# Turning the gated activations of a feed-forward: TensorE transposes replaced by VectorE blocks and two DMA transfers

## The chip, the cores and the metric

The kernel runs on one core of a Trainium2 chip. The metric is the device time of one execution in microseconds. Three runs of the kernel before took 1472.68, 1473.67 and 1474.22 us; their median, 1473.67 us, is the time before. One further execution was taken with the hardware profiler; every row of a profile below is from that one.

## The reference, cut to what matters

Two layers of an encoder, each of four blocks in a row: a feed-forward, a mixer of three attention-like branches, a cross-attention, and a second feed-forward. There are 256 tokens of width 1024; all data is fp32. The change touches the feed-forward alone, which is run four times:

```
def swiglu(h, w13, w2):
    gate, up = jnp.split(h @ w13, 2, axis=-1)
    return (jax.nn.silu(gate) * up) @ w2

h = rms_norm(x, ffn1_norms[l, 0])
x = x + 0.5 * rms_norm(swiglu(h, ffn1_w13[l], ffn1_w2[l]), ffn1_norms[l, 1])
```

with w13 of shape (1024, 5632) and w2 of shape (2816, 1024). The product silu(gate) * up, a matrix of 256 tokens by 2816, has its tokens on the partitions when it is computed; the product with w2 sums over the 2816 and so needs them on the partitions.

## The kernel before, in words

The 256 tokens are two tiles of 128 (i = 0, 1). Every fp32 product is made of three matmuls: each operand is split into a high part h and a low part l (`split`: ScalarE writes h as a rounded copy, VectorE writes l = value - h), and `mm3` adds h·h, h·l and l·h in PSUM. These are lines 210, 211 and 215, and nearly all of TensorE's work; one such matmul has 128 rows of weights and 512 columns.

The weights come from one stream in DRAM, in blocks of 128 x 1024. `load` takes a block: the SP queue brings it into `raw` (4 buffers), ScalarE makes `wh` (line 156) and VectorE `wl` (line 157), 8 buffers each. A block is used by 12 matmuls, then its buffers come free for the block eight further on.

A feed-forward (`ffn`) goes over the 2816 in six chunks: chunk 0 of 256 columns, chunks 1 to 5 of 512. In a chunk, `gemm_chunk` makes gate (4 blocks, 24 matmuls for each i) and up (the same). Then `gated` computes `s` = silu(gate) on ScalarE (line 363) and `g` = up * s on VectorE (line 365), and defers to the next `tick` the call `into_T`: TensorE transposes `g` in pieces of 128 x 128 (line 262; four for a chunk of 512, two for one of 256) into PSUM, from which `split` makes `gTh` and `gTl`. After up of chunk c come the rows of w2 of chunk c - 1, which use `gT` of chunk c - 1: four blocks of 12 matmuls. Behind chunk 5 stands `finish`: eight rows of w2 are left, of chunks 4 and 5. Two are done for both i (24 matmuls), and then the last six together for i = 0 and then for i = 1, for each half n of the output; the rows of chunk 4 come first in each. `boundary` then makes the norm and the new x.

A scheduler orders the instructions of each engine by dependence and priority when the kernel is built, and sets the waits. Each engine runs its own instructions strictly in that order, a DMA that it issues included.

Of the kernel before, what the change touches and what calls it, by code (L numbers as in the profile page):

```python
# [11 lines left out]
F32 = mybir.dt.float32  # L12
# [8 lines left out]
P = 128  # L21
# [33 lines left out]
def _ffn_blocks(f, l):  # L55
    w13, w2 = f"{f}_w13", f"{f}_w2"
    out = {("w13", 0): _chunk(w13, (l,), [(2560, 2816), (D_FF + 2560, D_FF + 2816)]), ("w2", 0): [_kn(w2, (l,), k, 1, [(0, D)]) for k in (20, 21)]}
    for c in range(1, 6):
        o = (c - 1) * 512
        out["g", c] = _chunk(w13, (l,), [(o, o + 512)])  # L60
        out["u", c] = _chunk(w13, (l,), [(D_FF + o, D_FF + o + 512)])
        out["w2", c] = [_kn(w2, (l,), 4 * (c - 1) + k, 1, [(0, D)]) for k in range(4)]
    return out
# [3 lines left out]
    return [_kn(name, idx, k, 1, [(0, D)]) for k in range(nk)]  # L67


def _lay(inputs, blk):  # L70
    name, idx, k0, nk, cols = blk
    w = inputs[name][idx]
    parts = [w[k0 * P:(k0 + nk) * P, a:b].reshape(nk, P, b - a) for a, b in cols]
    a = np.concatenate(parts, axis=2) if len(parts) > 1 else parts[0]
    return np.ascontiguousarray(a.transpose(1, 0, 2)).reshape(-1)
# [28 lines left out]
def hybrid_encoder(ctx: ExitStack, tc: tile.TileContext, stream: Stream, t: dict, out: bass.AP):  # L104
    nc = tc.nc
# [6 lines left out]
    wk = ctx.enter_context(tc.tile_pool(name="wk", bufs=2))  # L112
    st = ctx.enter_context(tc.tile_pool(name="st", bufs=48))
    xp = ctx.enter_context(tc.tile_pool(name="xp", bufs=1))
    pps = ctx.enter_context(tc.tile_pool(name="pps", bufs=8, space=PSUM))

    def ps_tile():
        return pps.tile([P, 512], F32, tag="ps", name="ps")
# [34 lines left out]
    def split(h, l, src, scale=None):  # L153

        if scale is None:
            nc.scalar.activation(h, src, AF.Copy)  # L156
            nc.vector.tensor_tensor(out=l, in0=src, in1=h.bitcast(F32), op=ALU.subtract)  # L157
        else:
            nc.scalar.activation(h, src, AF.Copy, scale=scale)
            nc.vector.scalar_tensor_tensor(out=l, in0=src, scalar=scale, in1=h.bitcast(F32), op0=ALU.mult, op1=ALU.subtract)  # L160

    def load(blk):

        blk = _freeze(blk)
        w = _blk_width(blk)
        off = stream.place(blk)
        raw = wp.tile([P, w], F32, tag="raw", name="raw", padded_shape=[P, BLK])
        nc.sync.dma_start(out=raw, in_=ws[off:off + P * w].rearrange("(p e) -> p e", p=P))
        h = hp.tile([P, w], F32R, tag="wh", name="wh", padded_shape=[P, BLK])
        l = hp.tile([P, w], F32R, tag="wl", name="wl", padded_shape=[P, BLK])  # L170
        split(h, l, raw)
        nk = blk[3]
        return (h.rearrange("p (k n) -> p k n", k=nk), l.rearrange("p (k n) -> p k n", k=nk))
# [3 lines left out]
    def defer(fn, pieces=1):  # L177

        queue.append(fn if pieces == 1 else lambda: defer(fn, pieces - 1))

    def tick():
        due = queue[:]
        queue.clear()
        for fn in due:
            fn()
# [31 lines left out]
    def gemm_chunk(o, aT, blocks, j0=0, total=None, low_last=False):  # L217

        tiles = [(bh[:, k, :], bl[:, k, :]) for bh, bl in blocks for k in range(bh.shape[1])]
        total = total or len(tiles)  # L220
        for k, (bh, bl) in enumerate(tiles):
            j = j0 + k
            if low_last:
                mm2(o, aT[0][:, j, :], bh, bl, j == 0)
            else:
                mm3(o, aT[0][:, j, :], aT[1][:, j, :], bh, bl, j == 0, j == total - 1)
        for k, (bh, bl) in enumerate(tiles if low_last else []):
            nc.tensor.matmul(o, lhsT=aT[1][:, j0 + k, :], rhs=bh, start=False, stop=j0 + k == total - 1)  # L228
        tick()

    def lead(blks_a, use_a, blks_b, use_b, beside=lambda n: None):

        a = []
        for n, k in enumerate(blks_a):
            a.append(load(k))
            beside(n)
        o0, p0 = ps_tile(), ps_tile()
        gemm_chunk(o0, xT[0], a, low_last=True)
        use_a(0, o0)
        b = [load(k) for k in blks_b[:2]]  # L240
        gemm_chunk(p0, xT[0], b, 0, KD)
        o1 = ps_tile()
        gemm_chunk(o1, xT[1], a)
        use_a(1, o1)
        b += [load(k) for k in blks_b[2:]]
        gemm_chunk(p0, xT[0], b[2:], 4, KD)
        use_b(0, p0)
        p1 = ps_tile()
        gemm_chunk(p1, xT[1], b)
        use_b(1, p1)  # L250

    def gemm_rows(o, n, aT, j, blk, first, last):

        bh, bl = blk
        c = slice(n * 512, n * 512 + 512)
        mm3(o, aT[0][:, j, :], aT[1][:, j, :], bh[:, 0, c], bl[:, 0, c], first, last)

    def transposes(src, n, rows=P):

        p = ps_tile()  # L260
        for i in range(n):
            nc.tensor.transpose(p[:rows, i * P:(i + 1) * P], src[:, i * rows:(i + 1) * rows], ident)  # L262
        return p
# [6 lines left out]
    def into_T(dst, j0, src, nblk, scale=None):  # L270

        p = transposes(src, nblk)
        pv = p[:, :nblk * P].rearrange("p (k t) -> p k t", k=nblk)
        split(dst[0][:, j0:j0 + nblk, :], dst[1][:, j0:j0 + nblk, :], pv, scale)
# [46 lines left out]
    def new_accs():  # L321
        return [[ps_tile() for _ in range(2)] for _ in range(NT)]
# [32 lines left out]
    def ffn(f, l, r, pg, ng, early=lambda n: None, beside=lambda: None):  # L355
        b = _ffn_blocks(f, l)
        with tc.tile_pool(name="ff", bufs=2) as ff:
            gT = {}

            def gated(i, c, gate, up):  # L360
                w = gate.shape[1]
                s = ff.tile([P, 512], F32, tag="s", name="s")
                nc.scalar.activation(s[:, :w], gate, AF.Silu, scale=r[i])  # L363
                g = ff.tile([P, 512], F32, tag="g", name="g")
                nc.vector.scalar_tensor_tensor(out=g[:, :w], in0=up, scalar=r[i], in1=s[:, :w], op0=ALU.mult, op1=ALU.mult)  # L365
                nk = w // P
                gT[c, i] = d = tuple(ff.tile([P, 4, P], F32R, tag=f"gT{p}", name=f"gT{p}", bufs=5) for p in "hl")
                defer(lambda: into_T(d, 0, g, nk))

            gate = {}  # L370

            def use_gate(c):
                def use(i, o):
                    gate[c, i] = o
                return use

            lead(b["w13", 0], lambda i, o: gated(i, 0, o[:, :256], o[:, 256:]), b["g", 1], use_gate(1), early)
            accs = new_accs()
            for c in range(1, 6):
                if c > 1:  # L380
                    blocks = [load(k) for k in b["g", c]]
                    for i in range(NT):
                        gate[c, i] = ps_tile()
                        gemm_chunk(gate[c, i], xT[i], blocks)
                blocks = [load(k) for k in b["u", c]]
                for i in range(NT):
                    o = ps_tile()
                    gemm_chunk(o, xT[i], blocks)
                    gated(i, c, gate[c, i], o)
                if c < 5:  # L390
                    for n, k in enumerate(b["w2", c - 1]):
                        blk = load(k)
                        for i in range(NT):
                            for h in range(2):
                                gemm_rows(accs[i][h], h, gT[c - 1, i], n, blk, c == 1 and n == 0, False)
                        tick()
                if c == 2:
                    beside()
            work = []
            for c in (4, 5):  # L400
                aT = [gT[c, i] for i in range(NT)]
                work += [(aT, n, k) for n, k in enumerate(b["w2", c])]
            return finish(accs, work, pg, ng, 4.0)
# [579 lines left out]
    for l in range(DEPTH):  # L983
        g = {k: t[f"{k}_norms"][l] for k in ("ffn1", "mix", "cross", "ffn2")}
        r = ffn("ffn1", l, r, g["ffn1"][1], g["mix"][0], *((early, rope_tables) if l == 0 else ()))
        r, mem = mixer(l, r, g["mix"][1], g["cross"][0])
        r = cross(l, r, mem, g["cross"][1], g["ffn2"][0])
        r = ffn("ffn2", l, r, g["ffn2"][1], t["ffn1_norms"][l + 1, 0] if l + 1 < DEPTH else None)
# [61 lines left out]
```

## Time and profile before

| | before |
|---|---|
| median of three runs | 1473.67 us |
| the profiled execution | 1472.88 us |
| its span in the profile | 1471.1 us |
| TensorE busy | 1452.0 us, 99% |
| VectorE busy | 895.7 us, 61% |
| ScalarE busy | 755.9 us, 51% |
| DMA of the main queue, share of 16 engines | 54.9% |
| transposes of g (line 262) | 176 |

A row of the profile names a line, an engine, an operation and its tiles as out<-in with their shapes. PE is TensorE's matmul, PEld its weight load, which runs beside the matmul before; DVE is VectorE, ACT ScalarE, POOL GpSimd, SPq the queue of SyncE. Matmuls overlap in the profile: each is shown 0.39 us long, and the next one starts 0.23 us after it, so the distance of two starts is what one costs, not its length.

### The profile page before, as it was taken

The page shows a single profiled execution, that of the slowest core. Times are in us where ns is not written, and L with a number is a line of the kernel's source. Part 1 is how long each engine was busy: PE and PEld are TensorE (multiplying, and loading weights), DVE is VectorE, ACT ScalarE, POOL GpSimd, SP SyncE. Part 2 cuts the span into 40 slices and gives each one's busy share as a digit, 9 for nine tenths or more (in the row PEclk, how much of TensorE's full clock was granted, in tenths as well). Part 3 has the DMA queues.
Part 4 walks back from the last instruction along what each step waited for, and adds up shares of the span by engine and source line. Part 5 has one row for each costly group of instructions (what it writes and reads, how often), then busy time and mean ns, then how long its engine had stood idle before and what let it go on. Part 6 is the DMA issues. An engine that isn't in the chain of part 4 may idle for free.

```text
span 1471.1 us, 18753 instructions
## 1 busy us (share of the span) xinstructions
PE 1452.0 (99%) x6988; PEld 1209.8 (82%) x6988; DVE 895.7 (61%) x1154; ACT 755.9 (51%) x1096; POOL 91.6 (6%) x192
## 2 busy tenths in 40 slices
PE   7999999999999999999999999999999999999998
PEld 6888888888788888888888888888887888888886
DVE  6655567465776657554575554765666866664553
ACT  6444455664546546444464443666554656554442
POOL 0000022100201001000000000221002010100000
PEclk9999999999999999999999999999999999999999
DMA  8656656444456527555466554655444664465561
GB/s 287 208 182 199 194 183 199 159 160 137 141 200 229 171 96 246 203 191 186 145 231 209 189 187 157 211 181 170 144 161 131 205 234 131 146 217 182 175 198 56
DMA packets 75756, 266.03 MB, mean 181 GB/s; under 512 B 8909, under 2 KB 10893, under 8 KB 75661
## 3 DMA queue, kind: packets, MB, share of 16 engines
q1 hardware_dynamic: 75664, 264.83, 54.9%
q8 instruction: 55, 0.90, 0.3%
q14 instruction: 37, 0.30, 0.1%
HBM read 263.75 MB, written 1.05 MB: 180 GB/s over the span
## 4 chain that ended last, share of the span: by engine, by line
PE 91%; DVE 3%; DMA 1%; ACT 1%; POOL 1%; issue 1%; SPq 0%; POOLq 0%; DVEq 0%; ACTq 0%
PE ps L210 28%; PE ps L211 28%; PE ps L215 28%; PE ps L262 4%; DMA raw<-in_ws 1%; DVE wl L157 1%; PE ps L761 1%; PE ps L781 1%; PE ps L228 1%; POOL st L143 0%; ACT wh L156 0%; PE ps L773 0%; ACT e L487 0%; DVE tg L583 0%; PE ps L934 0%
## 5 line engine op out<-in xcount | busy, mean ns | idle before, releaser
L157 DVE TENSOR_TENSOR wl<-raw,wh 128x1024 fp32r<-128x1024 f32 x478 | 577.2, 1217 | 310.7 <-ACT wh L156 296.7
L156 ACT ACTIVATE wh<-raw 128x1024 fp32r<-128x1024 f32 x478 | 502.0, 1056 | 372.7 <-PE ps L215 323.0
L210 PE MATMUL ps<-wh,xTh 128*128 128x512 f32 (+1 forms) x1312 | 519.0, 396 | 0.5 <-ACT mem L156 0.5
L211 PE MATMUL ps<-wl,xTh 128*128 128x512 f32 (+1 forms) x1312 | 511.4, 390 | 1.9 <-DVE wl L157 1.9
L215 PE MATMUL ps<-wh,xTl 128*128 128x512 f32 (+1 forms) x1264 | 491.7, 389 | 0.0
L211 PEld LDWEIGHTS ps<-wl,xTh 128*128 128x128 f32 x1312 | 247.4, 189 | 51.3 <-DVE wl L157 3.6
L210 PEld LDWEIGHTS ps<-wh,xTh 128*128 128x128 f32 x1312 | 247.3, 189 | 50.2 <-ACT mem L156 0.9
L215 PEld LDWEIGHTS ps<-wh,xTl 128*128 128x128 f32 x1264 | 237.2, 188 | 49.3 <-DVE xTl L160 0.2
L210 PE MATMUL ps<-wh,gTh 128*128 128x512 f32 x352 | 141.3, 401 | 0.0
L215 PE MATMUL ps<-wh,gTl 128*128 128x512 f32 x352 | 137.5, 391 | 0.0
L211 PE MATMUL ps<-wl,gTh 128*128 128x512 f32 x352 | 137.0, 389 | 0.0
L215 PEld LDWEIGHTS ps<-wh,gTl 128*128 128x128 f32 x352 | 66.0, 188 | 14.5
L211 PEld LDWEIGHTS ps<-wl,gTh 128*128 128x128 f32 x352 | 66.3, 188 | 12.5
L210 PEld LDWEIGHTS ps<-wh,gTh 128*128 128x128 f32 x352 | 66.2, 188 | 12.2
L363 ACT ACTIVATE s<-ps,st 128x512 f32<-128x512 f32 (+1 forms) x48 | 31.4, 654 | 82.1 <-PE ps L215 78.7
L300 POOL TENSOR_SCALAR st<-st 128x1 f32<-128x1 f32 x16 | 4.8, 302 | 969.3 <-ACT junk L294 969.3
L365 DVE SCALAR_TENSOR_TENSOR g<-ps,st,s 128x512 f32<-128x512 f32 (+1 forms) x48 | 33.7, 703 | 49.1 <-PE ps L215 48.4
L296 DVE TENSOR_TENSOR t<-ps,gain 128x512 f32<-128x512 f32 x32 | 22.0, 689 | 56.4 <-ACT junk L294 56.4
L487 ACT ACTIVATE e<-ps,st 128x256 f32<-128x256 f32 (+1 forms) x80 | 33.5, 430 | 34.6 <-DVE st L485 34.6
L210 PE MATMUL ps<-wh,mem 128*128 128x512 f32 x128 | 51.0, 398 | 0.0
L215 PE MATMUL ps<-wh,mem 128*128 128x512 f32 x128 | 50.0, 390 | 0.0
L211 PE MATMUL ps<-wl,mem 128*128 128x512 f32 x128 | 49.9, 390 | 0.0
(202 smaller groups left out, 1302.4 us busy)
## 6 DMA issues: line engine op xcount, KB each, us to landing
raw<-in_ws SPq DMA_DIRECT2D x466, 512.0 KB, 4.3
gain<-in_ffn_norms SPq DMA_DIRECT2D x7, 512.0 KB, 5.4
raw<-in_ws SPq DMA_DIRECT2D x8, 416.0 KB, 5.2
gain<-in_mix_norms SPq DMA_DIRECT2D x4, 512.0 KB, 4.9
gain<-in_cross_norms SPq DMA_DIRECT2D x4, 512.0 KB, 5.1
m<-in_mem SPq DMA_DIRECT2D x4, 512.0 KB, 3.6
raw<-in_ws SPq DMA_DIRECT2D x4, 384.0 KB, 3.0
tmpb<-in_c_decay SPq DMA_DIRECT2D x8, 192.0 KB, 3.4
```

Source lines behind the costliest of these rows:

```text
L156: nc.scalar.activation(h, src, AF.Copy)
L157: nc.vector.tensor_tensor(out=l, in0=src, in1=h.bitcast(F32), op=ALU.subtract)
L210: nc.tensor.matmul(o, lhsT=ah, rhs=bh, start=first, stop=False)
L211: nc.tensor.matmul(o, lhsT=ah, rhs=bl, start=False, stop=False)
L215: nc.tensor.matmul(o, lhsT=al, rhs=bh, start=False, stop=last)
L228: nc.tensor.matmul(o, lhsT=aT[1][:, j0 + k, :], rhs=bh, start=False, stop=j0 + k == total - 1)
L262: nc.tensor.transpose(p[:rows, i * P:(i + 1) * P], src[:, i * rows:(i + 1) * rows], ident)
L296: nc.vector.tensor_tensor(out=tt[h], in0=y[h], in1=pg[:, cc], op=ALU.mult)
L363: nc.scalar.activation(s[:, :w], gate, AF.Silu, scale=r[i])
L365: nc.vector.scalar_tensor_tensor(out=g[:, :w], in0=up, scalar=r[i], in1=s[:, :w], op0=ALU.mult, op1=ALU.mult)
L487: nc.scalar.activation(e[:, h, :w], s[:, j, :], AF.Exp, bias=nm[:, h:h + 1], accum_out=sums[:, h:h + 1])
L761: nc.tensor.matmul(s[h], lhsT=qT[i][:, 4 * g + h, :], rhs=kT[:, 4 * g + h, :w], start=True, stop=True)
```

## The change

`gated` no longer defers `into_T`; it calls `turn`. VectorE transposes `g` in blocks of 32 x 32 into `gB`. ScalarE's queue writes `gB` to a tile `far` in DRAM (128 rows of 2 KB for a chunk of 512). At the next tick the same queue reads `far` back into `gM` with rows and pieces exchanged (for each partition four pieces of 512 bytes), and at the tick after that `split` makes `gTh` and `gTl` from `gM`, in SBUF. In `gT` the 128 features of a block stand in another order than before; on the host, the rows of w2 are put in the same order (`_turned`). TensorE's transposes in other parts of the kernel stay.

```
+def _turned(w):
+    n = w.shape[-1]
+    return w.reshape(-1, 4, 32, n).transpose(0, 2, 1, 3).reshape(-1, n)
...
+    if name in ("ffn1_w2", "ffn2_w2"):
+        w = _turned(w)
...
+    dram = ctx.enter_context(tc.tile_pool(name="dram", bufs=4, space=bass.MemoryType.DRAM))
...
+            def turn(dst, src, nk):
+                b = ff.tile([P, 512], F32, tag="gB", name="gB")[:, :nk * P]
+                nc.vector.transpose(b.rearrange("p (c k t) -> p k c t", c=4, t=32), src.rearrange("p (k c j) -> p k c j", k=nk, c=4))
+                far = dram.tile([4, P, nk, 32], F32, tag=f"far{nk}", name="far")
+                nc.scalar.dma_start(out=far.rearrange("a (j c) k t -> (a j) (c k t)", c=4), in_=b)
+
+                def back():
+                    m = ff.tile([P, 512], F32, tag="gM", name="gM")[:, :nk * P].rearrange("p (a e) -> p a e", a=4)
+                    nc.scalar.dma_start(out=m, in_=far.rearrange("a q k t -> q a (k t)"))
+                    h, l = (d[:, :nk, :].rearrange("p k (a t) -> p a k t", a=4) for d in dst)
+                    defer(lambda: split(h, l, m.rearrange("p a (k t) -> p a k t", t=32)))
+                defer(back)
...
-                defer(lambda: into_T(d, 0, g, nk))
+                turn(d, g[:, :w], nk)
```

The scheduler's order on TensorE at the end of the first feed-forward, before: the four transposes of `g` of chunk 5, i = 0, stand between the last matmul of up (on xT) and the first of w2's row (on gT); line 262 is the transpose.

```order
L211 MATMUL ps<-wl,xTh_90 128x512
L215 MATMUL ps<-wh,xTl_91 128x512
L262 MATMUL ps<-ident,g 128x128 [waits DVE_49,Activation_49]
L262 MATMUL ps<-ident,g 128x128 x3
L210 MATMUL ps<-wh,gTh 128x512 [waits Activation_49]
```

The same place on TensorE after (the lines are 9 further down in the file):

```order
L220 MATMUL ps<-wl,xTh_92 128x512
L224 MATMUL ps<-wh,xTl_93 128x512
L219 MATMUL ps<-wh,gTh 128x512 [waits Activation_49]
L220 MATMUL ps<-wl,gTh 128x512 [waits DVE_49]
L224 MATMUL ps<-wh,gTl 128x512
```

The transposes are gone; the matmuls around them keep their order, here and (but for two single matmuls that change places with a neighbour) in the whole program.

ScalarE's order at the same place, from the silu of chunk 5, i = 1, to the first square of `boundary` (line 294 before, 303 after), before:

```order
L363 ACTIVATE s_1426<-ps_1314,st_227 128x512
L156 ACTIVATE wh_1487<-raw_1485 128x1024
L156 ACTIVATE wh_1493<-raw_1491 128x1024
L156 ACTIVATE wh_1499<-raw_1497 128x1024
L156 ACTIVATE wh_1505<-raw_1503 128x1024
L156 ACTIVATE wh_1511<-raw_1509 128x1024
L156 ACTIVATE gTh_1392<-ps_1419 128x512
L156 ACTIVATE wh_1698<-raw_1696 128x1024
L156 ACTIVATE gTh_1430<-ps_1454 128x512
L156 ACTIVATE wh_1704<-raw_1702 128x1024
L294 ACTIVATE junk_1534,st_1533<-ps_320 128x512
```

After, at the same place:

```order
L165 ACTIVATE wh_1511<-raw_1509 128x1024
L377 DMA far_1412<-gB_1410 128x512
L165 ACTIVATE wh_1517<-raw_1515 128x1024
L165 ACTIVATE wh_1523<-raw_1521 128x1024
L381 DMA gM_1439<-far_1412 128x4x128
L165 ACTIVATE wh_1529<-raw_1527 128x1024
L165 ACTIVATE gTh_1408<-gM_1439 128x4x4x32
L165 ACTIVATE wh_1716<-raw_1714 128x1024
L377 DMA far_1449<-gB_1447 128x512
L165 ACTIVATE wh_1722<-raw_1720 128x1024
L381 DMA gM_1475<-far_1449 128x4x128
L165 ACTIVATE gTh_1445<-gM_1475 128x4x4x32
```

For each of the two `gTh` two DMA issues now stand in ScalarE's order, with one or two splits of weights (`wh`) between them; the second pair stands behind the first `gTh`. The row behind the last one is the square, as before.

## Rows read from the trace of the kernel before

**Rows 1.** The page: busy time, share of the span and instructions; clock by slices.

```profile
PE 1452.0 (99%) x6988; PEld 1209.8 (82%) x6988; DVE 895.7 (61%) x1154; ACT 755.9 (51%) x1096; POOL 91.6 (6%) x192
...
PEclk9999999999999999999999999999999999999999
```

**Rows 2.** The page: the chain that ended last, by engine.

```profile
PE 91%; DVE 3%; DMA 1%; ACT 1%; POOL 1%; issue 1%; SPq 0%; POOLq 0%; DVEq 0%; ACTq 0%
```

**Rows 3.** Groups by line and shape: busy us, mean ns of one, idle before.

```profile
L262 PE MATMUL ps<-ident,g 128*128 128x128 f32 x176 | 27.1, 272 | 1.2 <-DVE g L365 1.1
...
L157 DVE TENSOR_TENSOR wl<-raw,wh 128x1024 fp32r<-128x1024 f32 x466 | 565.1, 1223 | 302.2 <-ACT wh L156 288.5
...
L774 DVE COPY pT<-ps 128x512 f32<-128x512 f32 x12 | 7.9, 683 | 7.8 <-PE ps L773 7.8
```

**Rows 4.** Timeline of PE about four transposes: start us, us.

```profile
109.20 0.40 PE L215 MATMUL ps<-wh,xTl 128*128 128x512 f32 x1
...
109.44 0.60 PE L262 MATMUL ps<-ident,g 128*128 128x128 f32 x4
...
109.80 0.48 PE L210 MATMUL ps<-wh,gTh 128*128 128x512 f32 x1
...
110.11 0.40 PE L211 MATMUL ps<-wl,gTh 128*128 128x512 f32 x1
```

**Rows 5.** Timeline of PE about two transposes (chunk 0, i = 1).

```profile
569.14 0.40 PE L215 MATMUL ps<-wh,xTl 128*128 128x512 f32 x1
569.37 0.38 PE L262 MATMUL ps<-ident,g 128*128 128x128 f32 x2
569.51 0.48 PE L210 MATMUL ps<-wh,xTh 128*128 128x512 f32 x1
569.83 0.40 PE L211 MATMUL ps<-wl,xTh 128*128 128x512 f32 x1
```

**Rows 6.** Timeline of PE, chunk 0, i = 0, of both second feed-forwards.

```profile
560.53 0.48 PE L210 MATMUL ps<-wh,xTh 128*128 128x512 f32 x1
561.13 0.44 PE L262 MATMUL ps<-ident,g 128*128 128x128 f32 x2
...
1286.64 0.48 PE L210 MATMUL ps<-wh,xTh 128*128 128x512 f32 x1
1288.18 0.44 PE L262 MATMUL ps<-ident,g 128*128 128x128 f32 x2 [1.06 <-DVE g L365]
```

**Rows 7.** Busy time in a stretch, one chunk: us, then each engine, clock, DMA.

```profile
109.00:143.00 34.00, 34.00 (x155) 28.12 (x154) 17.58 (x18) 15.31 (x17) 0.00 (x0) 1.00 0.60 188
```

**Rows 8.** DMA: the main queue's packets, MB and share; KB, us to landing.

```profile
q1 hardware_dynamic: 75664, 264.83, 54.9%
...
raw<-in_ws SPq DMA_DIRECT2D x466, 512.0 KB, 4.3
...
out_dram<-x SPq DMA_DIRECT2D x4, 256.0 KB, 2.0
```

**Rows 9.** Tile x: issue of a DMA of it, and all its landings.

```profile
L978 SPq DMA_DIRECT2D x<-in_x x1: 432/432/432, 2.6 to 2.6; - x1
...
DMA to landing us min/median/max: 2.0/2.8/4.7
```

**Rows 10.** Timeline of ACT and DVE, end of the first feed-forward.

```profile
172.71 1.06 ACT L156 ACTIVATE wh<-raw 128x1024 fp32r<-128x1024 f32 x1 [5.16 <-PE ps L215]
...
176.79 1.06 ACT L156 ACTIVATE wh<-raw 128x1024 fp32r<-128x1024 f32 x1 [0.30 <-PE ps L215]
...
187.26 0.60 ACT L294 ACTIVATE junk<-ps 128x512 bf16<-128x512 f32 x1 [3.02 <-PE ps L215]
...
171.35 0.75 DVE L365 SCALAR_TENSOR_TENSOR g<-ps,st,s 128x512 f32<-128x512 f32 x1 [2.54 <-PE ps L215]
...
178.37 0.69 DVE L157 TENSOR_TENSOR gTl<-ps,gTh 128x512 fp32r<-128x512 f32 x1
```

**Rows 11.** DMA activity in 40 slices of 172 to 182 us.

```profile
DMA  4321000000000000998779939695899899999966
```

## Prediction

> **What bounds the kernel now.** I read the busy times first: TensorE 99%, VectorE 61%, ScalarE 51% [rows 1]. Matmuls overlap in the profile, so 99% alone proves little; the chain that ended last confirms it: 91% of the span is TensorE's, no other engine has over 3% [rows 2]. The granted clock is at full speed in all 40 slices [rows 1], which is the upper of its two levels, 2.4 GHz, so there is no clock to win. Whatever leaves TensorE's order in a stretch where it never waits is therefore won in full, as long as no wait takes its place. One chunk of a feed-forward, 109 to 143 us, shows how much room the others have: of 34.0 us VectorE works 17.6, ScalarE 15.3, and the DMA engines 60% [rows 7].
>
> **What it removes.** 176 transposes of g [rows 3]: in each feed-forward ten groups of four and two of two. The price is a distance of starts. Matmuls stand 0.23 us apart (569.14 to 569.37). From the matmul before a group of four, 109.20, to the second matmul after it, 110.11, is 0.91 us; without the group it would be 0.46, so four cost 0.45 us [rows 4]. For two: 569.14 to 569.83 is 0.69, so 0.23 [rows 5]. Sum: 40 x 0.45 + 8 x 0.23 = 18.0 + 1.9 = 19.9 us. At two places TensorE also waits for g ahead of the pair: 560.53 to 561.13 is 0.60 instead of 0.23, and 1286.64 to 1288.18 is 1.54 [rows 6], 1.7 us in all. What stands next there after the change does not read g; unless xT is just as late, this is won too. Bounds 0 and 1.7; I take 1.5, since only g is named as the releaser. Together 21.4.
>
> **What it adds on VectorE.** 48 block transposes of 128x512 or half that. No such operation is in the trace. The nearest row is the copy of 128x512, 0.68 us; above it I put the 1.22 us of an operation with twice the elements [rows 3]. Two a chunk are 1.4 to 2.4 us, in 16.4 us of free time. What stands behind them is the split of weights, `wl`. A block of weights that comes free in the first quarter of up's pass for i = 1 is needed again 18 + 48 matmuls later, 15.0 us; its two splits take 1.06 [rows 10] and 1.22 us [rows 3], so 12.7 us are spare. Cost: nothing. The split of g itself moves from PSUM to SBUF at the same size; I keep its 0.69 us [rows 10].
>
> **What it adds on ScalarE's queue.** Four DMA issues a chunk. SP pays 0.43 us for one [rows 9], so 1.7 us in some 18 us of free time. The issues are not the matter; the waits are, because ScalarE runs in order: `far` waits for VectorE's block transpose, `gM` for `far` to land, `gTh` for `gM`. In the order, the i = 1 pair stands behind the first `gTh`, so a chunk has four hops (h each) one after another, with five splits of weights in between (5.3 us). A hop carries 256 KB. Rows for it: the output, 256 KB in the same rows of 2 KB, lands in 2.0 us [rows 8], on a quiet queue; the tile x lands in 2.0 at least, 2.8 in the middle, 4.7 at most [rows 9]; a weight block, twice the bytes, in 4.3 among its like [rows 8]. I take 2.8, and 2.0 to 4.7 as bounds. The reads come in 512 packets of 512 bytes, 32 for each of the 16 DMA engines. A packet of the main queue takes on average 0.549 x 16 x 1471 / 75664 = 0.171 us for 3.5 KB [rows 8]; if a small one took as long, a read would need 5.5 us instead of the 0.8 us that its bytes need at the same rate (264.83 MB in 54.9% of 1471 us, 328 GB/s). I take the bytes for nearer, as a weight block of 128 packets lands in 4.3 us and not in proportion to packets; the 5.5 goes into the rivals.
>
> **In the middle of a chunk** this hides. ScalarE's work is 15.3 + 1.7 us, the four hops add 4h - 5.3; at h = 2.8 that is 22.9 of 32.6 us. Single weight splits come late by 3 to 5 us, against 12.7 spare.
>
> **At the end of a feed-forward** it is tight, for there gT of chunk 5 is used at once. Take the first one, in which up of chunk 5 ends at 176.79 (the last of its four blocks is freed) [rows 10]. `gTh` for i = 0 is needed after 24 + 6 matmuls, at 183.6, `gTl` 0.4 later; for i = 1 after 66, at 191.8. After the change g is done at 172.1 and its block transpose at about 173; `far` goes out behind the split that starts at 172.71, at 173.8 [rows 10]; `gM` after the landing, at 176.6; `gTh` at 176.6 + 2.8 + 0.6 = 180.0. Spare: 3.6 us. Then a split of 1.06, `far`, `gM`, and the second `gTh` is done at 180.0 + 1.06 + 5.6 + 0.6 = 187.3; spare 4.5. The square of `boundary` behind it started at 187.26 after 3.0 us of idling [rows 10], so nothing is pushed. In general the second is done at 176.1 + 4h: it becomes late above h = 3.9, the first above 4.6. The first read, though, meets traffic: the DMA engines are idle from 173 to 176 us and then 70 to 90% busy to the end of the rows [rows 11], with the next stage's weights. Four blocks of 1.6 us from 176.2 on plus the read's 0.8 put its landing at 183.4 at the latest, its `gTh` at 184.0 and `gTl` at 184.7: at most 0.7 us late, and 0 at best. With the receipt of the last packet I allow 1.3. In three feed-forwards that is 0 to 4 us (behind the last no weights follow); I take 2.
>
> **Sum**, against the profiled execution's 1472.88: 1472.88 - 18.0 - 1.9 - 1.5 + 2 = 1453.5. That execution lies 0.8 us under the median of the runs, so a median would read about 1454; I forecast 1454.
>
> One rule speaks against the change. The Trainium skill, "VectorE: DVE Perf Modes", section "Rules for kernel authors", gives a 128 x 128 transpose to TensorE or to the crossbar DMA and leaves VectorE the 32 x 32 one. What TensorE's transposes cost here is shown above by rows; by that rule alone the 19.9 us would be well spent and the sum would stay at 1472.88.
>
> **The rivals.**
>
> *The end of a feed-forward is late.* If h is above 3.9 us there, by contention or small packets, each microsecond more costs 4 us of TensorE in each feed-forward. At 4.7: 4 x 0.8 x 4 = 12.8 us, so 1472.9 - 21.4 + 12.8 = 1464. For it: the busy stretch in [rows 11]. Against: far and gM of i = 1 fall where the weights of the next stage have mostly arrived, and a blocked ScalarE itself holds back the next loads.
>
> *ScalarE becomes the bound: slower.* In a chunk 15.3 + 1.7 + 4h - 5.3 passes 32.6 us above h = 5.2; from there each microsecond of h costs 4 us in each of 20 chunks, 80 us. At h = 5.5 all is eaten; at h = 6 the kernel takes 1472.9 - 21.4 + 64 = 1515 us. For it: packets priced by count would give a read of 2.0 + 5.5 = 7.5 us, with writes at 2.8 a mean just at the edge, 5.2. Against: [rows 8, 9], where no landing of half a block comes near. The Trainium skill, "VectorE: DVE Perf Modes", section "The three transpose paths", warns that a plain DMA that transposes by strides is 19 times slower than the crossbar when the innermost stride at the destination is large. No run here shows that; the innermost run of both transfers is contiguous, 2 KB or 512 bytes, so I don't add to this rival's chance for it.
>
> *Nothing to be seen:* h between the two, such that the ends give back 18 to 24 us. It needs h of 5.0 to 5.4.
>
> **How the numbers follow.** Hidden but for a little: 0.70, from 1450.5 (both waits won, no loss) to 1457. Late ends: 0.16, from 1457 to 1470.7. No change: 0.04. ScalarE the bound: 0.10, above 1476.6. About 0.2%, 2.9 us, is what a measurement of this kernel can tell from no change. The range 1450 to 1463 holds the first case and two thirds of the second. Faster 0.86, same 0.04, slower 0.10.
>
> **What would show each step.** The span of a chunk falls from 33.5 by 0.9 us, with the matmuls 0.23 us apart and no row of g among them: the removal is right. ScalarE's waits name DMA far and DMA gM, a few us a chunk, and TensorE's waits stay under 1 us outside the ends: hidden. A wait of TensorE for `gTh` or `gTl` in the last 15 us of a feed-forward: the first rival, and its length is the price. TensorE waiting for `wh` or `wl` inside chunks: the second. Landings of far and gM give h; above 3.9 us I am wrong on the ends, above 5.2 on the sign.

## The result, and the profile after

The changed kernel took 1455.49 us (median of four runs, 1455.10 to 1456.78). The kernel before took 1473.18 (four runs, three of them those of the table above). The ratio is 0.988, 95% interval 0.9868 to 0.9893: 1.2% faster, 17.7 us. The forecast was 1454 us in a range of 1450 to 1463. The profiled execution of the changed kernel was the longest of its four runs, 1456.78 us with a span of 1455.0.

The page of the changed kernel, the lines that answer to [rows 1, 2, 8]: busy times, clock in slices, ScalarE's own DMA queue (q10; packets, MB, share), the chain that ended last by engine, and the DMA landings (KB each, us):

```profile
PE 1432.2 (98%) x6812; PEld 1191.8 (82%) x6812; DVE 923.7 (63%) x1202; ACT 753.7 (52%) x1096; POOL 90.9 (6%) x192
...
PEclk9999999999999999999999999999999999999999
...
q10 hardware_dynamic: 32256, 23.07, 4.9%
...
PE 89%; DMA 4%; DVE 3%; ACT 2%; issue 1%; POOL 1%; SPq 0%; POOLq 0%; DVEq 0%; ACTq 0%
...
far<-gB ACTq DMA_DIRECT2D x40, 256.0 KB, 2.7
gM<-far ACTq DMA_DIRECT2D x40, 256.0 KB, 4.6
```

TensorE has 176 matmuls less and is still the bound. DMA has come into the chain, with 4%. Of the two transfers the write lands in 2.7 us, next to the 2.8 that was assumed; the read takes 4.6, just under the upper bound of 4.7.

TensorE's timeline of the changed kernel at the place of [rows 4], and at the end of the first feed-forward (start us, us):

```profile
108.29 0.39 PE L224 MATMUL ps<-wh,xTl 128*128 128x512 f32 x1
...
108.74 0.39 PE L220 MATMUL ps<-wl,gTh 128*128 128x512 f32 x1
...
196.03 0.60 PE L271 MATMUL ps<-ident,xg 128*128 128x128 f32 x4
197.33 0.50 PE L219 MATMUL ps<-wh,xTh 128*128 128x512 f32 x1 [0.70 <-ACT xTh L165]
```

From the last matmul of up to the second on gT there are now 0.45 us where [rows 4] had 0.91. The last two rows show the one kind of place where TensorE now waits and did not before: the transposes of xg for the mixer, and behind them a matmul that starts 1.30 us later and waits for xTh.

The waits of the changed kernel, TensorE's and ScalarE's (us in total, times, longest us):

```profile
PE ps L220 <- DVE wl L166: 2.5, 3, 1.5
...
PE ps L219 <- ACT xTh L165: 2.3, 3, 0.8
...
ACT gTh L165 <- DMA gM<-far: 144.4, 47, 7.2
ACT wh L165 <- DMA far<-gB: 47.7, 22, 4.3
```

ScalarE stands still 192 us before the two transfers, and TensorE has no row of a wait for gTh or gTl. The wait for xTh comes three times, once behind each feed-forward that has something after it.

VectorE's groups of the changed kernel by line and shape, the block transpose (busy us, mean ns of one, idle before):

```profile
L375 DVE STREAM_TRANSPOSE gB<-g 128x512 f32<-128x512 f32 x40 | 28.3, 708 | 0.7
```

**Where the time went.** A matmul of the one program can be found in the other, and the difference of its two starts followed through the span (minus: earlier after). Its steps in the two profiled executions, in us:

```
start, first tiles of x                       +1.22
40 groups of four, 0.45 to 0.50 each         -19.06
the pairs of chunk 0, with the waits for g    -3.25
ends of feed-forwards 1, 2, 3 (4: none)       +3.67   (1.13 + 1.19 + 1.35)
mixers of the two layers                      +1.29   (0.60 + 0.69)
sum                                          -16.13
```

The start differs between runs of one kernel: the second tile of x let TensorE begin at 7.27 us before, at 8.41 after, and at 7.27 to 8.4 in the traces below, whatever they do with g. The mixers' part is also not the change's: in a second profile of the changed kernel it is 0.0 and at most -0.2. The ends are there again, at 1.06, 0.80 and 1.07. So three terms are left: the transposes, the waits for g, and the ends. Inside the chunks the steps are those of the groups alone: no time is lost there.

### The profile page after: what moved, and what is told of

It reads as the page before. It is cut to its first block, busy times and chain, and to the rows that moved or that the text cites. A ratio compares the mean times of both kernels' runs of the same rounds, so it can differ in the third digit from the quotient of the medians.

```text
span 1455.0 us, 18558 instructions
## 1 busy us (share of the span) xinstructions
PE 1432.2 (98%) x6812; PEld 1191.8 (82%) x6812; DVE 923.7 (63%) x1202; ACT 753.7 (52%) x1096; POOL 90.9 (6%) x192
## 3 DMA queue, kind: packets, MB, share of 16 engines
q10 hardware_dynamic: 32256, 23.07, 4.9%
## 4 chain that ended last, share of the span: by engine, by line
PE 89%; DMA 4%; DVE 3%; ACT 2%; issue 1%; POOL 1%; SPq 0%; POOLq 0%; DVEq 0%; ACTq 0%
PE ps L219 28%; PE ps L220 28%; PE ps L224 27%; PE ps L271 3%; DMA raw<-in_ws 1%; DMA gM<-far 1%; DVE wl L166 1%; ACT wh L165 1%; PE ps L237 1%; PE ps L787 1%; PE ps L807 1%; DMA far<-gB 1%; POOL st L152 1%; PE ps L799 0%; DVE tg L609 0%
## 5 line engine op out<-in xcount | busy, mean ns | idle before, releaser
L219 PE MATMUL ps<-wh,gTh 128*128 128x512 f32 x352 | 137.2, 390 | 0.0
L165 ACT ACTIVATE gTh<-gM 128x512 fp32r<-128x512 f32 (+1 forms) x48 | 28.7, 597 | 144.5 <-DMA gM<-far 144.4
L166 DVE TENSOR_TENSOR gTl<-gM,gTh 128x512 fp32r<-128x512 f32 (+1 forms) x48 | 30.9, 643 | 96.6 <-ACT gTh L165 96.6
```

Of the source, the lines that this page charges most:

```text
L219: nc.tensor.matmul(o, lhsT=ah, rhs=bh, start=first, stop=False)
```

## The experiments

The theory after reading the trace: each group of transposes cost what the distance of starts says; what the new route costs TensorE lies only at the ends. ScalarE's timeline of the changed kernel at the end of the first feed-forward shows how (start us, us; ACTq rows are the issues of DMAs, in brackets the idle time before and its releaser):

```profile
170.09 0.33 ACTq L377 DMA_DIRECT2D far<-gB  x1
...
172.71 0.38 ACTq L381 DMA_DIRECT2D gM<-far  x1
...
176.54 0.63 ACT L165 ACTIVATE gTh<-gM 128x512 fp32r<-128x512 f32 x1 [1.43 <-DMA gM<-far]
...
177.45 0.33 ACTq L377 DMA_DIRECT2D far<-gB  x1
...
182.73 0.38 ACTq L381 DMA_DIRECT2D gM<-far  x1
187.56 0.63 ACT L165 ACTIVATE gTh<-gM 128x512 fp32r<-128x512 f32 x1 [7.02 <-DMA gM<-far]
188.10 0.58 ACT L303 ACTIVATE junk<-ps 128x512 bf16<-128x512 f32 x1
...
188.80 0.60 ACT L303 ACTIVATE junk<-ps 128x512 bf16<-128x512 f32 x1
```

The four hops, from one of these rows to the next, are 2.6, 3.8, 5.3 and 4.8 us. The second gTh comes at 187.56, and both squares of `boundary` follow without a gap. Before, the squares started at 187.26 [rows 10] and, in the same timeline of the kernel before, at 191.40:

```profile
191.40 0.60 ACT L294 ACTIVATE junk<-ps 128x512 bf16<-128x512 f32 x1 [3.45 <-PE ps L215]
```

TensorE runs 3.74 us earlier here, so they were due at 183.52 and 187.66. The second is 1.14 us late, and behind it hang the norm, the new x, xg and xTh: the loss of 1.13. On TensorE the first matmuls that read the two gTh of chunk 5 start at

```profile
180.60 0.39 PE L219 MATMUL ps<-wh,gTh 128*128 128x512 f32 x1
...
188.76 0.39 PE L219 MATMUL ps<-wh,gTh 128*128 128x512 f32 x1
```

and neither waits: the two gTh are done at 177.17 and 188.19.

### Without the transposition: the ceiling

```
-                turn(d, g[:, :w], nk)
+                defer(lambda: split(*(x[:, :nk, :] for x in d),
+                                    g[:, :w].rearrange("p (k t) -> p k t", k=nk)))
```

> Leaves the transposition of g out altogether: gT is split straight from g, no block transpose, no transfer (so the numbers it computes are not the reference's). It is the ceiling of the change. Theory (TensorE's transposes cost 0.45 us a group of four and 0.23 a pair, 20.2 us in all; what the route costs is only some 1.2 us at the end of each of three feed-forwards, where the second gT of the last chunk holds up the squares behind it on ScalarE): 1455.5 - 3.6 = 1452, between 1451 and 1453, and no wait of TensorE for xTh at the ends. Rival 1 (the route costs nothing, the small losses at the ends are noise or belong to the missing transposes): 1455.5. Rival 2 (the route also costs TensorE time spread through the chunks, by transfers that get in the way of the weights): clearly under 1451.

Measured: 1451.15 us (ratio 0.9851, 0.9836 to 0.9865). The squares start at 182.66 and 186.80, each as soon as TensorE is done, and the three ends lose 0.0 us each. The forecast of 1452 holds, and by the medians the whole route costs 4.3 us against not turning g at all, 3.7 of them at the ends.

### Order alone: the first square ahead of the second gTh

```
+            sq.append(nc.scalar.activation(junk[:, :512], y[h], AF.Square, scale=math.sqrt(c / D), accum_out=parts[h]).ins)
...
+                    def late():
+                        with tc.issue_after(sq[-1]):
+                            split(h, l, m.rearrange("p a (k t) -> p a k t", t=32))
+                    if last:
+                        defer(late, 3)
...
-                turn(d, g[:, :w], nk)
+                turn(d, g[:, :w], nk, (c, i) == (5, 1))
```

> Only the order at the end of a feed-forward changes: the split of the second gT of chunk 5 (gTh, gTl) is put behind boundary's first square of i = 0 on ScalarE, where it stood ahead of both squares. Theory (both squares are held up by gTh, and the second one by 1.14 us): the first square starts at about 183.5 us of the trace instead of 188.1, the second at 188.1 instead of 188.8, so 0.7 us of the 1.1 to 1.3 lost at each of three ends comes back: about 2 us, 1453.4, between 1452.5 and 1454.5. Rival (the ends lose because the next stage's weights or the transfers come late, whatever ScalarE's order is): 1455.5, TensorE's wait for xTh unchanged.

Measured: 1452.42 us (1451.36 to 1453.80; ratio 0.9857, 0.984 to 0.9873). ScalarE's timeline of this kernel at the end of the first feed-forward:

```profile
183.57 0.60 ACT L305 ACTIVATE junk<-ps 128x512 bf16<-128x512 f32 x1 [2.97 <-PE ps L224]
...
187.31 0.63 ACT L165 ACTIVATE gTh<-gM 128x512 fp32r<-128x512 f32 x1 [3.06 <-DMA gM<-far]
187.85 0.58 ACT L305 ACTIVATE junk<-ps 128x512 bf16<-128x512 f32 x1
```

gTh comes when it came before; only the first square has left its shadow. The ends lose 0.10, 0.29 and 0.73 us instead of 1.13, 1.19 and 1.35, and the wait for xTh is gone from TensorE's list. The landing was not changed, so it is the order on ScalarE that makes a late landing cost time. The gain, 3 us, is just beyond the edge of what was expected (1452.5).

### GpSimd's queue instead of ScalarE's

```
-                nc.scalar.dma_start(out=far.rearrange("a (j c) k t -> (a j) (c k t)", c=4), in_=b)
+                nc.gpsimd.dma_start(out=far.rearrange("a (j c) k t -> (a j) (c k t)", c=4), in_=b)
...
-                    nc.scalar.dma_start(out=m, in_=far.rearrange("a q k t -> q a (k t)"))
+                    nc.gpsimd.dma_start(out=m, in_=far.rearrange("a q k t -> q a (k t)"))
```

> Both transfers of the turn are issued by GpSimd instead of ScalarE, in all chunks. ScalarE no longer waits for far, only for gM. Theory (in the middle of a chunk ScalarE's waits are hidden, and at the end it is the sum of two landings that makes gTh late, whoever issues them): 1455.5 plus or minus 1.5, by how the landings from this queue differ; a microsecond more in the two hops of i = 1 costs about 1 us at each of three ends. Rival (ScalarE that stands in front of far keeps weight splits and so loads back, and that is what the ends and the mixers lose): 1452. Second rival (GpSimd's own issue is much slower): 1460 or more, with TensorE waiting for gTh or gTl.

Measured: 1460.53 us (1457.19 to 1461.52; ratio 0.991, 0.9895 to 0.9925), 5 us slower than ScalarE's queue and beyond the 1454 to 1457 that were expected. The landings on this kernel's page, and the second gTh in ScalarE's timeline at the first end:

```profile
far<-gB POOLq DMA_DIRECT2D x40, 256.0 KB, 4.8
gM<-far POOLq DMA_DIRECT2D x40, 256.0 KB, 5.7
```

```profile
190.95 0.63 ACT L165 ACTIVATE gTh<-gM 128x512 fp32r<-128x512 f32 x1 [7.11 <-DMA gM<-far]
```

ScalarE no longer waits for far, and nothing was won by it; but the landings grew at the same time, so what speaks against the first rival is the run before this one, where ScalarE stands in front of far as ever and most of the loss is gone. Two hops are 3.2 us longer (4.8 + 5.7 against 2.7 + 4.6); the issues on the engine are 0.6 of that (0.56 and 0.75 us instead of 0.33 and 0.38). The second gTh is 3.4 us later, but TensorE itself is 1.9 us later there, most of it from one place inside a chunk, at 102 us, where it waits 0.61 us for wh and 0.77 for wl. Against TensorE gTh is 1.5 us later, and the first end loses 2.5 us instead of 1.1: about the 1 us per us that was expected. The three ends lose 2.5, 2.0 and 3.0 us. Some of that stands as waits for gTh itself (2.1 us in all, 3 times). Together with a time above 1460 this is what the second rival named, though more by slow landings than by a slow issue.

### SP's queue, among the loads

The same two lines with `nc.sync`. The scheduler puts the first square ahead of the second gTh here too.

> Both transfers stand on SP's queue, among the loads of weights; ScalarE waits for gM alone, and a load stands behind far's and gM's waits. ScalarE's order has the first square ahead of the second gTh. Theory (loads run far enough ahead that a wait of SP of 3 to 6 us four times in a chunk does no harm; the ends gain as the order of the squares does): 1453, between 1452 and 1456. Rival (SP in front of gB and far keeps the loads back: a chunk's 16 to 20 loads need 60% of the DMA engines' time, and four stops of 4 to 5 us leave too little): 1480 or more, with TensorE waiting for wh and wl.

Measured: 1451.66 us (ratio 0.9854, 0.9838 to 0.9869), just under the 1452 to 1456 that were expected, and as good as no transposition at all. The landings on this kernel's page, and ScalarE's timeline at the first end:

```profile
far<-gB SPq DMA_DIRECT2D x40, 256.0 KB, 2.3
gM<-far SPq DMA_DIRECT2D x40, 256.0 KB, 4.1
```

```profile
183.44 0.60 ACT L303 ACTIVATE junk<-ps 128x512 bf16<-128x512 f32 x1 [3.02 <-PE ps L224]
...
184.64 0.63 ACT L165 ACTIVATE gTh<-gM 128x512 fp32r<-128x512 f32 x1 [0.51 <-DMA gM<-far]
187.58 0.60 ACT L303 ACTIVATE junk<-ps 128x512 bf16<-128x512 f32 x1 [2.31 <-PE ps L224]
```

Both squares now wait for TensorE alone, gTh is there 2.9 us earlier than in the changed kernel, and the ends lose 0.0 us. Order and queue both changed here; the order alone, in the run above, left 1.1 us of loss at the ends. SP stands 116 us in front of far, waiting for gB, and 38 us in front of gM, waiting for far, without harm: it waits 900 us for a free buffer anyway. Run again beside the changed kernel on one chip:

> The changed kernel once more, unedited, on the same chip and beside the next kernel, so that the two can be compared: 1455.5, between 1454.5 and 1456.5.

> The kernel with both transfers on SP's queue once more, beside the changed kernel. Theory (its whole gain is at the ends of three feed-forwards, where the first square stands ahead of the second gTh and that gTh is there 3 us earlier): 1451.7, between 1451 and 1452.5, 3 to 4.5 us under the changed kernel of the same chip. Rival (the difference lay in the chip or in chance): less than 1.5 us under it.

Measured: 1454.58 us for the changed kernel (ratio 0.9865, 0.9852 to 0.9879), 1451.08 for this one (five runs, 1451.04 to 1451.31; ratio 0.9843, 0.983 to 0.9857): 3.5 us less, inside what was expected. It is the fastest complete version of this study.

### Chunk 5 by TensorE again

```
+        w = np.concatenate([_turned(w[:2048]), w[2048:2560], _turned(w[2560:])])
...
+                if c == 5:
+                    defer(lambda: into_T(d, 0, g, nk))
+                else:
+                    turn(d, g[:, :w], nk)
```

> Chunk 5 of each feed-forward is transposed by TensorE again (its rows of w2 in the old order); the other chunks go by VectorE and DRAM. Theory: eight groups of four come back at 0.455 us, plus 3.6 us; the losses at the three ends go, minus 3.6 us: 1455.5, between 1454.5 and 1456.5, and no wait for xTh above those of the kernel before. Rival 1 (the losses at the ends have nothing to do with the hops of chunk 5): 1459. Rival 2 (transposes at the end of a feed-forward cost less than in its middle, since something else waits there): 1452.

Measured: 1455.35 us (ratio 0.9878, 0.9864 to 0.9893); the three ends lose 0.0 us and the time is that of the changed kernel. Eight groups of four came back and cost what the ends had cost. This is the same price from the other side, with both rivals 3 to 4 us away.

### Rows of 2 KB in the read

```
-                    nc.scalar.dma_start(out=m, in_=far.rearrange("a q k t -> q a (k t)"))
+                    nc.scalar.dma_start(out=m.rearrange("p a e -> p (a e)"),
+                        in_=far.rearrange("a (j c) k t -> (a j) (c k t)", c=4))
```

> The read back takes rows of 2 KB in the order in which they were written, 128 packets instead of 512; the same bytes. It leaves out the exchange of the four pieces, so features stand in the wrong order. Theory A (the read takes 4.6 us against the write's 2.7 because of its 512 small packets): gM lands in 2.7 to 3.0 us, ScalarE's waits for gM fall from 144 to about 55 us, the second gTh of a last chunk comes 1.5 to 2 us earlier, the ends lose nothing: 1452, between 1451 and 1453. Theory B (a read from DRAM takes longer than a write whatever its rows): gM stays at 4.3 to 4.8 us, the time at 1455.5.

Measured: 1454.83 us (ratio 0.9873, 0.9855 to 0.989), no different. The page of this kernel, its queue and the read's landing:

```profile
q10 hardware_dynamic: 13824, 23.07, 4.5%
...
gM<-far ACTq DMA_DIRECT2D x40, 256.0 KB, 4.5
```

The packets fall from 32256 to 13824, and the read still takes 4.5 us. Theory A falls: packets of 512 bytes are not why the read is slower. B, that a read is slower than a write, is not shown by it: in the kernel with two more hops, below, the write far takes 5.0 us and the last read 3.6. One thing that goes with the landing can be read in the changed kernel's own trace. Its rows for the last two hops of the first feed-forward and of the fourth, behind which no weights follow (us, busy times of the five engines, clock, DMA share, GB/s):

```profile
177.45:182.73 5.28, 5.28 (x25) 4.38 (x24) 2.99 (x3) 1.74 (x2) 0.00 (x0) 1.00 0.98 344
182.73:187.56 4.83, 4.83 (x23) 4.01 (x22) 0.00 (x0) 0.00 (x0) 0.00 (x0) 1.00 0.60 192
1430.38:1432.43 2.05, 2.05 (x11) 1.70 (x10) 0.54 (x1) 0.00 (x0) 0.00 (x0) 1.00 0.34 128
1432.43:1435.36 2.93, 2.93 (x15) 2.42 (x14) 0.00 (x0) 0.00 (x0) 0.00 (x0) 1.00 0.32 89
```

Among the next stage's weights the two hops take 5.3 and 4.8 us, without them 2.1 and 2.9. The share alone does not set them: on SP's queue the same two hops of the first feed-forward take 3.6 and 3.7 us at shares of 1.00 and 0.86. No run changed the traffic alone, so how the two work together stays open.

### Transposes put back on TensorE, beside the route

```
                 turn(d, g[:, :w], nk)
+                defer(lambda: transposes(g, nk))
```

> The whole changed kernel, and in addition TensorE transposes g as before into a PSUM tile that nobody reads (176 transposes, 48 groups). It prices the removed transposes by themselves, with the route in place. Theory (40 groups at 0.45 and 8 at 0.23 us, all of it in TensorE's own order): 1455.5 + 20.2 = 1475.7, between 1474.5 and 1477.5; it may get back a part of the 3.6 us of the ends, since TensorE's work there gives the hops more time: not under 1473. Rival (a part of the gain came from elsewhere, such as the waits for PSUM tiles or for g): 1470 or less.

Measured: 1485.87 us (1483.52 to 1490.91; ratio 1.009, 1.0067 to 1.0113), 10 us above the forecast. Its waits, ScalarE's and TensorE's timelines in the first chunk 0, and the clock in two stretches there (us, busy times, clock, DMA share, GB/s):

```profile
PE ps L271 <- DVE g L391: 10.6, 7, 3.2
```

```profile
31.60 2.00 ACT L165 ACTIVATE wh<-raw 128x1024 fp32r<-128x1024 f32 x2 [4.08 <-DMA far<-gB]
...
34.42 0.46 ACT L389 ACTIVATE s<-ps,st 128x256 f32<-128x256 f32 x1
...
35.84 0.69 PE L271 MATMUL ps<-ident,g 128*128 128x128 f32 x2 [3.21 <-DVE g L391]
36.17 0.78 PE L219 MATMUL ps<-wh,xTh 128*128 128x512 f32 x1
36.75 0.63 PE L220 MATMUL ps<-wl,xTh 128*128 128x512 f32 x1
```

```profile
30.00:32.40 2.40, 2.40 (x12) 1.85 (x10) 0.00 (x0) 0.80 (x1) 0.00 (x0) 1.00 0.93 330
36.00:38.90 2.90, 2.90 (x9) 2.34 (x10) 2.73 (x9) 0.40 (x1) 0.00 (x0) 0.51 0.84 263
```

ScalarE stands 4.08 us until far has landed; the silu of i = 1 is queued behind it and comes at 34.42, its g at 35.3, and TensorE, which reads g again here, stands still for 3.21 us until 35.84. So the route makes g late as well. In the changed kernel nobody feels it, since nothing but the route reads g. To take this out, the same transposes of something that is always there:

```
+                defer(lambda: transposes(x[i][:, :w], nk))
```

> The changed kernel with 176 transposes put back on TensorE at the places where those of g stood, but of x, which is there all the time, into a PSUM tile that nobody reads. The run with transposes of g put back came out 10 us above 1475.7; its trace shows TensorE waiting 10.6 us for g in chunk 0, where the silu that makes g stands on ScalarE behind the wait for far. Theory (the transposes by themselves cost 0.45 a group of four and 0.23 a pair; the rest of that run was the wait for a g that the route makes late, and the slower matmuls behind that wait): 1475.7, between 1474 and 1477. Rival (48 more PSUM tiles in turn, or the transposes' place among the matmuls of a kernel with the route, cost the 10 us): 1483 or more.

Measured: 1474.43 us (ten runs, 1472.19 to 1475.21; ratio 1.0009, 0.9999 to 1.0018), level with the kernel before. By the medians it lies 1474.43 - 1455.49 = 18.9 us above the changed kernel. That is not the price of the transposes alone, for the wait for xTh at the ends is gone with them: by the starts, against the changed kernel's profile, the groups put back cost 20.6 us and the three ends give back 2.8 (1.1, 0.8, 0.9). So the 20.2 us that were expected for the transposes are met, the time is inside the 1474 to 1477, and the rival of 1483 falls; what the ends give back, the expectation had left out.

### Two more hops

```
+                    far2 = dram.tile([4, P, nk, 32], F32, tag=f"fur{nk}", name="fur")
+                    nc.scalar.dma_start(out=far2.rearrange("a q k t -> q a (k t)"), in_=m)
+                    m2 = ff.tile([P, 512], F32, tag="gN", name="gN")[:, :nk * P].rearrange("p (a e) -> p a e", a=4)
+                    nc.scalar.dma_start(out=m2, in_=far2.rearrange("a q k t -> q a (k t)"))
...
-                    defer(lambda: split(h, l, m.rearrange("p a (k t) -> p a k t", t=32)))
+                    defer(lambda: split(h, l, m2.rearrange("p a (k t) -> p a k t", t=32)))
```

> Two more hops for each g: what has come back goes out to DRAM once more and back, by ScalarE's queue, before the split. Theory (ScalarE stands in order in front of each landing, and a chunk holds 16.7 us of work and four hops less 5.3 us of splits): 14.8 us more of hops in each of 20 chunks, of which 6.4 us are still free: 20 x 8.4 = 168, and at the end of each of four feed-forwards the second gT comes 14 us late, 57 us: about 1680, between 1580 and 1720, with TensorE waiting for wh and wl inside the chunks. Rival (inside a chunk landings lie beside everything else, since gT is needed only a chunk later): only the ends pay, about 1512.

Measured: 1550.88 us (1547.07 to 1555.37; ratio 1.0528, 1.0496 to 1.056), below the 1580 that the theory's range began with and above the rival's 1512. The landings on its page, TensorE's wait for gTh, and ScalarE's timeline in the middle of a chunk:

```profile
far<-gB ACTq DMA_DIRECT2D x40, 256.0 KB, 5.0
...
gN<-fur ACTq DMA_DIRECT2D x40, 256.0 KB, 3.6
```

```profile
PE ps L219 <- ACT gTh L165: 65.0, 8, 14.8
```

```profile
127.87 0.37 ACTq L383 DMA_DIRECT2D fur<-gM  x1
...
128.39 0.53 ACTq L377 DMA_DIRECT2D far<-gB  x1
...
135.02 0.63 ACT L165 ACTIVATE gTh<-gN 128x512 fp32r<-128x512 f32 x1 [2.67 <-DMA gN<-fur]
```

The ends are as worked out: the starts of matched matmuls against the changed kernel lose 15, 17, 15 and 13 us there, 59 in all, where 57 was expected; 53 of the 65 us of waits for gTh lie there. The chunks lose some 40 us instead of 168, of which 12 are waits for gTh and some 14 waits for wl and wh. The sum of hops was taken for a queue, one after another; here far of i = 1 goes out at 128.39 while the chain of i = 0 still runs to 135.02, so the two chains overlap; ScalarE is busy for 48% of the span. This kernel's order is not that of the changed one (there the second far stands behind the first gTh), so it shows that the sum of hops is too hard a bound, not where the changed kernel's own bound lies.

## Why the prediction was right, step by step

**The removal** was worth what the starts say. The forecast was 19.9 us; the matched starts give 40 groups of 0.45 to 0.50, on average 0.477, and seven pairs of 0.21 to 0.24 (the first one is lost in the late start): 19.1 + 1.6 = 20.7. The group of [rows 4] was at the low end. The run with transposes of x put back agrees from the other side: 20.6 us by the starts, 18.9 by the medians after what the ends give back. The Trainium skill's rule cited against the change ("VectorE: DVE Perf Modes", section "Rules for kernel authors"), that a 128 x 128 transpose belongs on TensorE, does not hold for this kernel: TensorE is the bound, and VectorE and the queues had room.

**The waits for g** were forecast at 1.5 us. Of the steps in the starts, 0.61 at 561 us and 1.51 at 1288 us, the pairs take 0.23 and 0.24: 1.65 us of waits won.

**VectorE**: the block transpose takes 0.71 us, in the bounds of 0.68 to 1.22 and next to the copy. TensorE's wait for wl is 2.5 us in 3 places; before it was 1.9, in 3.

**ScalarE's issues** take 0.33 and 0.38 us instead of 0.43. **The hop** was taken as 2.8 us; the write has 2.7, the read 4.6. The reason given for small hops, bytes and not packets, stood the test of 2 KB rows; the size for the read did not.

**In the middle of a chunk** it hides, as said: of the 192 us that ScalarE stands before the transfers, TensorE feels only what falls on the ends.

**The end of a feed-forward** is the step that fails, though its 2 us covered half of the price. The danger was seen in the first read, and 2 us were taken for it; the first gTh was done at 177.17 and is read at 180.60, with 3.4 us to spare, next to the 3.6 of the prediction. Of the second chain the text said two things. Its transfers were to fall where the next weights have mostly arrived; its two hops took 5.3 and 4.8 us, longer than the first chain's 2.6 and 3.8, and the four together are 4.14 on average where h = 2.8 was taken. And the square behind it started at 187.26 after idling, "so nothing is pushed". That sets a start with the last two groups of transposes still in it beside a 187.3 that was reckoned without them; without them the square is due 0.96 us earlier and is pushed by 1 us at h = 2.8 too.

By the prediction's own formula the second gTh is done at 176.1 + 4h. With 4.14, and with TensorE 2.78 us ahead of the kernel before when up ends, that is 189.9; it was 188.2. So beside the hops the formula was 1.7 us too long: `far` went out 0.9 us before its reckoned place (173.8 less 2.78, against 170.09), and the second `far` 0.9 us behind the start of the first gTh, where 1.7 were put.

What was missing is that the squares, not gT, are late first. By the rows above, the second square starts four hops and 0.91 + 0.54 + 0.70 us after 170.09 and is due at 187.66, so it is late from h = 3.86 on; the second gTh is done four hops and 0.91 + 0.63 us after 170.09 and is read at 188.76, so it is late only from 4.28 on. The 4.14 lies between the two: TensorE waits for xTh and has no wait for gTh. So the ends cost 3.7 us where 2 were taken, through another wait. Behind the last feed-forward, where the hops are short, nothing is lost, as the prediction said.

**The sum**: 0.8 + 0.15 us more was won and 1.7 more lost than forecast, which nearly cancels. That is in part luck: the 2 us were taken for a read that was not late, and they stand near the price of a wait that the text had ruled out. The profiled execution has the late start and the mixers on top, 2.5 us that are not the change's; the median of the runs, 1455.49, lies 1.5 us above the forecast. One slip changes nothing: of the second case, 1457 to 1470.7, the range up to 1463 holds 6 of 13.7 us, which the text calls two thirds. Of the rivals, "the end is late" happened in its mechanism, a late second landing, at 3.7 us instead of the 6 to 20 that set it apart; "ScalarE becomes the bound" did not, and the run with two more hops shows that its threshold was worked out with hops in a row that need not be in a row.

## What to carry to other kernels

Work that leaves the engine that bounds the kernel is won at the distance of starts, and a detour of 7 us through DRAM was free here wherever the result is needed only a chunk later. Look for its price at the ends of stages, and there not first at the consumer of the data but at what stands behind the waiting instruction on its engine: here a norm of another tile. Moving one such instruction ahead of the wait, or the wait's transfers to a queue that idles anyway, gave back 3 to 4 us, and no run showed a price for it.

## What the runs showed of the hardware that was not expected

A stop of TensorE can cost more than its length. Behind the 3.2 us of waiting in the first chunk 0 of the run with g's transposes put back, six matmuls stand 0.41 to 0.58 us apart from start to start (the first two at 36.17 and 36.75) instead of 0.23, and the granted clock of 36.0 to 38.9 us is 0.51, the lower of the two levels, against 1.00 from 30.0 to 32.4. By the starts that adds 1.3 us to the stop.

The same 256 KB land in 2.3 and 4.1 us from SP's queue, 2.7 and 4.6 from ScalarE's, 4.8 and 5.7 from GpSimd's. The Trainium skill, "DMA: Bandwidth & Descriptors", section "Issuing engine by pattern", calls the path of SyncE and ScalarE generally faster than that of GpSimd; the traces agree: from GpSimd's queue the write lands 2.1 us later than from ScalarE's and the read 1.1.
